# The second feed-forward matmul in seven groups of seven products, and low parts formed on GpSimd

## The chip, the core and the metric

The kernel runs on one core of a Trainium2 chip. Its engines work side by side, each through its own queue in order: TensorE (PE, its weight loads as PEld), VectorE (DVE), ScalarE (ACT), GpSimd (POOL) and SyncE (SP), which here issues the DMA transfers between main memory and the on-chip memory SBUF. TensorE accumulates into eight banks of a second memory, PSUM. The metric is device time in microseconds (us) of one execution; the time of a kernel is the median of its runs.

## What is computed

One layer over 512 positions of width 1024: a modulated norm, an input projection, two branches (a gated spatial mixing and a matrix-memory recurrence), their merge, an output projection, and then the part that the change touches:

```python
xn = modulate(rmsnorm(h, norm2_g[l]), sh2, sc2)
ff = jnp.square(jax.nn.relu(xn @ w_ff1[l])) @ w_ff2[l]
h = h + g2[:, None, :] * ff
...
return rmsnorm(h, final_g)
```

`w_ff2` has 4096 rows and 1024 columns. The second matmul is the product of the 512 x 4096 activations with it; its result is multiplied by the row `g2`, added to the residual, and the sum is normed and scaled by `final_g`.

## The kernel before

**Products in three parts.** Every f32 operand is split into a high part (a cast to fp32r, on ScalarE) and a low part (operand minus high part, on VectorE). `mm3` (lines 116 to 119) issues three matmuls: high by high, high by low, low by high. Of the tiles with names in the profile, `wh`/`wl` are the parts of weights and `hsh`/`hsl` those of activations.

**Groups.** The inner dimension of 4096 is cut into eight blocks of 512. `GROUPS = "WWWWWS"` (line 1013) says how the first six are done. The four quarters of the activations of block n are `hq[n, 0/1, 0/1]` (a11, a12, a21, a22, each 128 x 512 on chip), those of its weights are F11, F12, F21 and F22 (each 128 x 1024 on chip). A "W" block makes seven products of sums of quarters where the plain way makes eight; `passes` (lines 1103 to 1138) writes them out. For a W block it issues, beside the products, four sums of weights (lines 1115, 1123, 1127, 1131) and three of activations (1117 to 1119), all on VectorE. An "S" block makes the eight plain products in the same two passes. Pass 0 runs over all blocks and collects products P1, P2, P7 and P3, pass 1 runs over them again and collects P5, P6 and P4 (and, for the S block, E); the weight quarters that both passes need are loaded twice.

**A step** is one product: two rows of output by two inner slices by three matmuls, 12 matmuls with 512 columns each. For each step `hl` (lines 1091 to 1101) splits the activations, 128 x 512, and `w_pair` (1075 to 1086) the weights, 128 x 1024:

```python
act.copy(out=h_, in_=src)
dve.tensor_sub(out=l_, in0=src, in1=h_.bitcast(F32))
```

The loop at line 1206 calls `prefetch_step(5)`, so that the operands of five steps may be ready or under way. There are six buffers for split activations (after the first two), five for split weights and three or four for raw weights; a planner orders each engine's queue by estimated costs, within what the buffers allow.

**Collecting.** `after(key)` adds the collected products, which lie in PSUM, to `r` tiles in SBUF, on VectorE (lines 1181 to 1197). `gated` (1175 to 1179) multiplies an `r` tile by `g2` and adds it to the residual, two VectorE instructions of 128 x 512.

**The rest of the inner dimension,** rows 24 to 31 in units of 128 (`KF = 4 * NF` to `NK`), is done in plain pieces: `ff2_piece` loads one piece of 128 rows, ScalarE and VectorE split it, and `hs_pair` splits the matching activations. Four pieces are multiplied for all four row blocks at once (lines 1251 to 1258), with `gated` calls between them. The other four (`LAST = 4`) are kept and multiplied row block by row block in `mm_last` (1262), so that each row block can be finished (`add_out`, `square`, `scaled`, `root`, lines 1268 to 1304) while the next is multiplied. Row block 3 has its own ending (lines 1305 to 1328), whose upper half is cut into two parts of 256 columns.

**Elsewhere.** `evac_qk` (line 426), early in the kernel, is the one place before that forms a low part on GpSimd (line 439). The first feed-forward matmul (`product`, line 1000, and the sums behind it) runs just ahead of the stage. `load_split` (line 91) is the weight split of the earlier stages; its VectorE line is L96.

Of the kernel before, what the change touches and what calls it, by code (L numbers as in the profile page):

```python
# [8 lines left out]
F32 = mybir.dt.float32  # L9
F32R = mybir.dt.float32r  # L10
# [6 lines left out]
P = 128  # L17
D = 1024
T = 512
KT = D // P  # L20
TB = T // P
# [28 lines left out]
def block_kernel(ctx, tc, vecs_d, rows_d, ws_d, x_d, w_ada, w_in, w_out, w_ff1, w_ff2, out_d):  # L50
    nc = tc.nc
    act, dve, pool, pe, sp = nc.scalar, nc.vector, nc.gpsimd, nc.tensor, nc.sync
# [6 lines left out]
    def bank(nm):  # L59
        return psum.tile([P, 512], F32, tag="ps", name=nm)  # L60
# [55 lines left out]
    def mm3(out, ah, al, bh, bl, start, stop):  # L116
        pe.matmul(out, lhsT=ah, rhs=bh, start=start, stop=False)  # L117
        pe.matmul(out, lhsT=ah, rhs=bl, start=False, stop=False)  # L118
        pe.matmul(out, lhsT=al, rhs=bh, start=False, stop=stop)  # L119
# [487 lines left out]
    n = 0  # L607
# [182 lines left out]
    def halves(src, nm):  # L790
        hl = []
        for q in range(2):
            h_ = fp.tile([P, 512], F32R, tag="hT", name=f"{nm}h{q}", bufs=32)
            l_ = fp.tile([P, 512], F32R, tag="hT", name=f"{nm}l{q}", bufs=32)
            act.copy(out=h_, in_=src[q])
            dve.tensor_sub(out=l_, in0=src[q], in1=h_.bitcast(F32))
            hl.append((h_, l_))
        return hl
# [211 lines left out]
        prefetch_op(2)  # L1010
        return bk.rearrange("p (f t) -> p f t", f=2)

    GROUPS = "WWWWWS"

    def minus_a21(n):
        if GROUPS[n:n + 1] == "W":
# [74 lines left out]
    def hl(src):  # L1091
        i = count[1]
        count[1] += 1
        if i < 2:
            both = fp.tile([P, 2, 2, 256], F32R, tag="sc", name=f"hs0{i}", bufs=2)
            h_, l_ = both[:, 0], both[:, 1]
        else:
            h_, l_ = hs_tile("h"), hs_tile("l")
        act.copy(out=h_, in_=src)  # L1099
        dve.tensor_sub(out=l_, in0=src, in1=h_.bitcast(F32))  # L1100
        return h_, l_

    def passes():
# [55 lines left out]
    pass_pool.append(ps_stack.enter_context(tc.tile_pool(name="passes", bufs=1, side="right")))  # L1159
    for _ in range(4):  # L1160
        right.more()
    ws_ff = Stream([(w_ff2[k * P:(k + 1) * P, :], 1, D, f"f2{k}") for k in range(KF, NK - LAST)], 2)
    hsq = {}

    def hs_pair(kp):
        for th in range(2):
            hsq[kp, th] = hl(hq[kp // 2, kp % 2, th])
# [3 lines left out]
    def rtile(nm, t):  # L1171
        res[nm, t] = hsp.tile([P, 512], F32, name=f"r{nm}{t}")
        return res[nm, t]

    def gated(nm, t, row, hf):
        cs = slice(hf * 512, (hf + 1) * 512)
        r_ = res[nm, t]
        dve.tensor_mul(out=r_, in0=r_, in1=g2[:, cs])
        dve.tensor_add(out=xr[:, row, cs], in0=xr[:, row, cs], in1=r_)

    def after(key):
        for t in range(2):
            b_ = acc_b.get((key, t))
            if key == "P1":
                act.copy(out=rtile("1", t), in_=b_)
            elif key == "P7":
                dve.tensor_add(out=rtile("7", t), in0=res["1", t], in1=b_)
            elif key == "P3":
                dve.tensor_add(out=rtile("3", t), in0=res["1", t], in1=b_)
            elif key == "P2":  # L1190
                dve.tensor_add(out=res["1", t], in0=res["1", t], in1=b_)
            elif key == "P6":
                dve.tensor_add(out=res["3", t], in0=res["3", t], in1=b_)
                dve.tensor_add(out=res["7", t], in0=res["7", t], in1=b_)
            elif key == "P5":
                dve.tensor_add(out=res["3", t], in0=res["3", t], in1=b_)
                dve.tensor_add(out=rtile("5", t), in0=res["7", t], in1=b_)

    last_of = {key: max(i for i, p_ in enumerate(plan_) if p_[1] == key) for _, key in plan_}
    end0 = max(i for i, p_ in enumerate(plan_) if p_[0] == 0)  # L1200
    jobs = {}
    for i_, keys in ((last_of["P7"] + 2, ("P1", "P7")), (end0 + 2, ("P3", "P2")),
                     (last_of["P4"] if GROUPS[-1] == "W" else last_of["P6"] + 3, ("P6", "P5"))):
        jobs.setdefault(i_, []).extend(keys)
    NS = len(plan_)
    for i, (pas, key) in enumerate(plan_):
        prefetch_step(5)
        (h_, l_), (wh, wl) = ready.pop(0)
        first = (key, 0) not in acc_b
        for t in range(2):  # L1210
            if first:
                acc_b[key, t] = bank(f"g{key}{t}")
            ts_ = slice(t * P, (t + 1) * P)
            for j in range(2):
                mm3(acc_b[key, t], h_[:, j, ts_], l_[:, j, ts_], wh[:, j], wl[:, j], first and j == 0,
                    i == last_of[key] and j == 1 and key not in ("P4", "E"))
        for key_ in jobs.get(i, ()):
            after(key_)
        if i == end0:
            sp.dma_start(out=fing, in_=rows_d[5].partition_broadcast(P))  # L1220
        if NS - i <= 4:
            ws_ff.prefetch(max(0, 4 - (NS - i)))
        if i == NS - 2:
            hs_pair(KF // 2)

    ps_stack.close()
    lwp = ff.enter_context(tc.tile_pool(name="lwp", bufs=1, side="right"))
    o_banks = [[bank(f"ob{t}{hf}") for hf in range(2)] for t in range(2)]
    o_banks += [[acc_b["P4", t], acc_b["E", t]] for t in range(2)]
    late = [(nm, t, row + t, hf) for nm, row, hf in (("1", 0, 0), ("3", 0, 1), ("7", 2, 0), ("5", 2, 1)) for t in range(2)]  # L1230

    def ff2_piece(k, last=False):
        if last:
            raw = raws.tile([P, 1, D], F32, tag="raw", name=f"raw_f2{k}")
            sp.dma_start(out=raw[:, 0, :], in_=w_ff2[k * P:(k + 1) * P, :])
            wh = lwp.tile([P, 1, D], F32R, tag="lwh", name=f"wh_f2{k}", bufs=LAST)
            wl = lwp.tile([P, 1, D], F32R, tag="lwl", name=f"wl_f2{k}", bufs=LAST)
            act.copy(out=wh, in_=raw)
            dve.tensor_sub(out=wl, in0=raw, in1=wh.bitcast(F32))
        else:  # L1240
            wh, wl = ws_ff.next()
        if k % 2 == 0 and k > KF:
            hs_pair(k // 2)
        return wh, wl

    def mm_f2(k, t, hf, wh, wl, stop):
        cs = slice(hf * 512, (hf + 1) * 512)
        h_, l_ = (v[:, k % 2, (t % 2) * P:(t % 2 + 1) * P] for v in hsq[k // 2, t // 2])
        mm3(o_banks[t][hf], h_, l_, wh[:, 0, cs], wl[:, 0, cs], k == KF and t < 2, stop)

    for k in range(KF, NK - LAST):
        wh, wl = ff2_piece(k)
        for t in range(TB):
            for hf in range(2):
                mm_f2(k, t, hf, wh, wl, False)
        for _ in range(2):
            if late:
                gated(*late.pop(0))
    pcs = [ff2_piece(k, True) for k in range(NK - LAST, NK)]
    ss3 = fp.tile([P, TB, 3], F32, name="ss3")  # L1260
    rs3 = fp.tile([P, TB], F32, name="rs3")
    def mm_last(o, t, cs, start):
        for p_, (wh, wl) in enumerate(pcs):
            k_ = NK - LAST + p_
            h_, l_ = (v[:, k_ % 2, (t % 2) * P:(t % 2 + 1) * P] for v in hsq[k_ // 2, t // 2])
            mm3(o, h_, l_, wh[:, 0, cs], wl[:, 0, cs], start and p_ == 0, p_ == LAST - 1)

    def add_out(o, t, cs, nm):
        n = cs.stop - cs.start
        tmp = fp.tile([P, 512], F32, tag="tmp", name="ot" + nm, bufs=2)  # L1270
        dve.tensor_mul(out=tmp[:, 0:n], in0=o, in1=g2[:, cs])
        dve.tensor_add(out=xr[:, t, cs], in0=xr[:, t, cs], in1=tmp[:, 0:n])
# [1 line left out]
    def square(sc, t, cs, q):  # L1274
        act.activation(sc[:, cs], xr[:, t, cs], AF.Square, scale=1.0 / 32.0, accum_out=ss3[:, t, q:q + 1])

    def scaled(t, cs, nm):
        n = cs.stop - cs.start
        z = fp.tile([P, 512], F32, tag="hT", name="z" + nm, bufs=32)
        dve.tensor_mul(out=z[:, 0:n], in0=xr[:, t, cs], in1=fing[:, cs])  # L1280
        return z[:, 0:n]

    def root(t):
# [7 lines left out]
    for t in range(TB - 1):  # L1291
        sc = fp.tile([P, D], F32, tag="sc", name=f"sc3{t}", bufs=2)
        zs = []
        for hf, cs in enumerate((lo_, hi_)):
            mm_last(o_banks[t][hf], t, cs, False)
            add_out(o_banks[t][hf], t, cs, f"{hf}{t}")
            square(sc, t, cs, hf)
            if hf == 1:
                ss_sum(t)
            zs.append(scaled(t, cs, f"{hf}{t}"))  # L1300
        root(t)
        for z, cs in zip(zs, (lo_, hi_)):
            act.activation(xr[:, t, cs], z, AF.Copy, scale=rs3[:, t:t + 1])
            sp.dma_start(out=out_d[t * P:(t + 1) * P, cs], in_=xr[:, t, cs])
# [3 lines left out]
    mm_last(o_banks[t][0], t, lo_, False)  # L1308
    add_out(o_banks[t][0], t, lo_, "l0")
    square(sc, t, lo_, 0)  # L1310
    mm_last(o_banks[t][1][:, 0:256], t, c2, False)
    o_end = bank("obe")
    mm_last(o_end[:, 0:256], t, c3, True)
    add_out(o_banks[t][1], t, hi_, "l1")
    square(sc, t, c2, 1)
    ss_sum(t)
    add_out(o_end[:, 0:256], t, c3, "l2")
# [60 lines left out]
```

## Time and profile before

| what | value |
|---|---|
| time, median of 3 runs | 807.0 us (806.1 to 807.3) |
| the profiled execution | 806.75 us |
| its span in the profile | 805.0 us |
| TensorE busy, share of the span | 792.7 us, 98% |
| VectorE | 621.1 us, 77% |
| ScalarE | 404.2 us, 50% |
| GpSimd | 43.0 us, 5% |
| granted TensorE clock, mean | 0.994 of full |
| first matmul of the second feed-forward matmul | 636.03 us |
| last matmul of the kernel | 797.57 us |

Times in the profile count from the start of the span. A row in order of time has the start, the duration, the engine, the source line, the operation, "output <- inputs" by the program's names, the shapes, and how many such instructions it joins; in brackets the idle time before it and what ended it. A row of a group has the busy time and the mean duration in ns of one, and the idle time in front of them. Matmuls overlap, so that their spacing and not their duration gives their rate.

### The profile page before, as it was taken

The page shows a single profiled execution, that of the slowest core. Times are in us where ns is not written, and L with a number is a line of the kernel's source. Part 1 is how long each engine was busy: PE and PEld are TensorE (multiplying, and loading weights), DVE is VectorE, ACT ScalarE, POOL GpSimd, SP SyncE. Part 2 cuts the span into 40 slices and gives each one's busy share as a digit, 9 for nine tenths or more (in the row PEclk, how much of TensorE's full clock was granted, in tenths as well). Part 3 has the DMA queues.
Part 4 walks back from the last instruction along what each step waited for, and adds up shares of the span by engine and source line. Part 5 has one row for each costly group of instructions (what it writes and reads, how often), then busy time and mean ns, then how long its engine had stood idle before and what let it go on. Part 6 is the DMA issues. An engine that isn't in the chain of part 4 may idle for free.

```text
span 805.0 us, 11479 instructions
## 1 busy us (share of the span) xinstructions
PE 792.7 (98%) x4375; PEld 688.1 (85%) x4375; DVE 621.1 (77%) x938; ACT 404.2 (50%) x610; POOL 43.0 (5%) x62
## 2 busy tenths in 40 slices
PE   7999999999999999999999999999999999999996
PEld 6887888888988888888888899999999978888885
DVE  5889766774843348997847579888888799999966
ACT  5458566274533233242435247666666756646324
POOL 2004020121000000100000110000000000000000
PEclk8999999999999999999999999999999999999999
DMA  8974331143223388669337240333332466765302
GB/s 273 265 227 117 119 104 51 29 126 110 79 79 105 105 268 312 206 210 324 122 102 261 78 132 28 105 105 106 106 115 70 178 220 222 252 213 184 114 30 104
DMA packets 76423, 119.87 MB, mean 149 GB/s; under 512 B 5712, under 2 KB 38608, under 8 KB 76368
## 3 DMA queue, kind: packets, MB, share of 16 engines
q1 hardware_dynamic: 76368, 119.14, 46.6%
q8 instruction: 34, 0.56, 0.3%
q14 instruction: 21, 0.17, 0.1%
HBM read 117.02 MB, written 2.10 MB: 148 GB/s over the span
## 4 chain that ended last, share of the span: by engine, by line
PE 91%; DVE 2%; DMA 2%; ACT 2%; issue 1%; POOL 0%; SPq 0%; POOLq 0%; DVEq 0%
PE P L118 6%; PE P L117 6%; PE P L119 6%; PE gP L119 4%; PE gP L117 4%; PE gP L118 4%; PE qk L282 4%; PE wo L117 1%; PE wo L119 1%; PE wo L118 1%; PE cp L241 1%; PE k1b L117 1%; PE gb0b L118 1%; PE q1b L119 1%; PE gb0b L119 1%
## 5 line engine op out<-in xcount | busy, mean ns | idle before, releaser
L1099 ACT CAST hsh<-h 128x512 fp32r<-128x512 f32 x45 | 26.7, 620 | 26.9 <-PE gP L118 15.3
L1082 ACT CAST wh_g<-F 128x1024 fp32r<-128x1024 f32 x27 | 28.1, 1052 | 16.8 <-DVE F L1127 3.7
L119 PE MATMUL gP<-wh_g,hsl 128*128 128x512 f32 x92 | 35.8, 391 | 0.6 <-DVE hsl L1100 0.6
L118 PE MATMUL gP<-wl_g,hsh 128*128 128x512 f32 x92 | 35.8, 389 | 0.0
L117 PE MATMUL gP<-wh_g,hsh 128*128 128x512 f32 x92 | 35.7, 390 | 0.0
L1083 DVE TENSOR_TENSOR wl_g<-F,wh_g 128x1024 fp32r<-128x1024 f32 x27 | 32.9, 1225 | 0.8 <-ACT wh_g L1082 0.8
L921 ACT CAST wh_T<-T 128x1024 fp32r<-128x1024 f32 x21 | 22.0, 1048 | 20.0 <-PE P L118 18.4
L117 PE MATMUL P<-x2h,wh_B 128*128 128x256 f32 x112 | 31.6, 282 | 0.0
L118 PE MATMUL P<-x2l,wh_B 128*128 128x256 f32 x112 | 31.6, 282 | 0.0
L119 PE MATMUL P<-x2h,wl_B 128*128 128x256 f32 x112 | 31.6, 282 | 0.0
L921 ACT CAST wh_B<-B 128x1024 fp32r<-128x1024 f32 x21 | 22.0, 1049 | 16.4 <-PE P L118 15.4
L1100 DVE TENSOR_TENSOR hsl<-h,hsh 128x512 fp32r<-128x512 f32 x45 | 29.9, 692 | 0.3 <-ACT hsh L1099 0.3
L922 DVE TENSOR_TENSOR wl_T<-T,wh_T 128x1024 fp32r<-128x1024 f32 x21 | 25.7, 1224 | 3.0 <-ACT wh_T L921 2.9
L922 DVE TENSOR_TENSOR wl_B<-B,wh_B 128x1024 fp32r<-128x1024 f32 x21 | 25.6, 1220 | 0.0
L96 DVE TENSOR_TENSOR wl_gb<-raw_gb,wh_gb 128x1024 fp32r<-128x1024 f32 x8 | 9.8, 1224 | 19.7 <-ACT wh_gb L95 19.6
L118 PE MATMUL gP<-wl_x,hsh 128*128 128x512 f32 x64 | 24.9, 389 | 0.0
L117 PE MATMUL gP<-wh_x,hsh 128*128 128x512 f32 x64 | 24.9, 389 | 0.0
L119 PE MATMUL gP<-wh_x,hsl 128*128 128x512 f32 x64 | 24.9, 389 | 0.0
L667 DVE SCALAR_TENSOR_TENSOR accg<-arg,c_act,accg 128x1024 f32<-128x1024 f32 x14 | 18.0, 1283 | 6.5 <-DMA arg<-in_w_ada 6.3
L95 ACT CAST wh_ga<-raw_ga 128x1024 fp32r<-128x1024 f32 x8 | 8.4, 1052 | 27.2 <-PE ga0b L119 16.3
L976 ACT ACTIVATE h<-h 128x512 f32<-128x512 f32 x28 | 17.7, 632 | 8.5 <-DVE h L1036 4.0
L1082 ACT CAST wh_x<-F 128x1024 fp32r<-128x1024 f32 x16 | 16.6, 1050 | 9.5 <-DVE F L1115 3.9
(616 smaller groups left out, 2818.7 us busy)
## 6 DMA issues: line engine op xcount, KB each, us to landing
F<-in_w_ff SPq DMA_DIRECT2D x48, 512.0 KB, 4.2
B<-in_w_ff SPq DMA_DIRECT2D x28, 512.0 KB, 3.8
ar<-in_w_ada SPq DMA_DIRECT2D x64, 128.0 KB, 3.4
arg<-in_w_ada SPq DMA_DIRECT2D x16, 512.0 KB, 5.9
raw_f<-in_w_ff SPq DMA_DIRECT2D x12, 512.0 KB, 3.6
raw_o<-in_w_in SPq DMA_DIRECT2D x8, 512.0 KB, 4.1
raw_mv<-in_w_in SPq DMA_DIRECT2D x8, 512.0 KB, 3.6
raw_gb<-in_w_in SPq DMA_DIRECT2D x8, 512.0 KB, 3.7
```

What stands on the lines that cost most here:

```text
L117: pe.matmul(out, lhsT=ah, rhs=bh, start=start, stop=False)
L118: pe.matmul(out, lhsT=ah, rhs=bl, start=False, stop=False)
L119: pe.matmul(out, lhsT=al, rhs=bh, start=False, stop=stop)
L282: pe.matmul(bk, lhsT=wx[:, kk, f * P:(f + 1) * P], rhs=xx[k], start=k == 0 and ps_ == 0, stop=k == KT - 1 and ps_ == 2)
L667: dve.scalar_tensor_tensor(out=acc, in0=raw, scalar=c_act[:, k:k + 1], in1=acc, op0=ALU.mult, op1=ALU.add)
L921: act.copy(out=wh, in_=src)
L922: dve.tensor_sub(out=wl, in0=src, in1=wh.bitcast(F32))
L976: act.activation(dst, src, AF.Relu)
L1082: act.copy(out=wh, in_=src)
L1083: dve.tensor_sub(out=wl, in0=src, in1=wh.bitcast(F32))
L1099: act.copy(out=h_, in_=src)
L1100: dve.tensor_sub(out=l_, in0=src, in1=h_.bitcast(F32))
```

## The change

`GROUPS` becomes `"WWWWWWW"`: the sixth block becomes a W block, and rows 24 to 27 become a seventh. Only rows 28 to 31 stay as plain pieces. Their weights are loaded and split in the last five steps of the loop, by `last_piece`, as halves of 512 columns. The low part in `hl` is formed on GpSimd. The `gated` calls are placed anew: "1" some steps after pass 0, "3" on VectorE and "7" and "5" on GpSimd after the loop. The scaling with `final_g` of row blocks 1 and 2 goes to GpSimd too. P5 and P6 are collected after their own last steps. The bank E is no longer used; row blocks 2 and 3 take P4 and a new bank, and the row blocks 0 and 1 start on empty banks in `mm_last`. In row block 3, the upper half is added in two parts of 256 columns.

```diff
-    GROUPS = "WWWWWS"
+    GROUPS = "WWWWWWW"
...
         act.copy(out=h_, in_=src)
-        dve.tensor_sub(out=l_, in0=src, in1=h_.bitcast(F32))
+        pool.tensor_sub(out=l_, in0=src, in1=h_.bitcast(F32))
         return h_, l_
...
-    def gated(nm, t, row, hf):
+    def gated(nm, t, row, hf, eng=dve):
...
+    def last_piece(k):
+        raw = raws.tile([P, D], F32, tag="raw", name=f"raw_f2{k}")
+        sp.dma_start(out=raw, in_=w_ff2[k * P:(k + 1) * P, :])
+        return halves([raw[:, 0:512], raw[:, 512:1024]], f"f2{k}")
...
-                     (last_of["P4"] if GROUPS[-1] == "W" else last_of["P6"] + 3, ("P6", "P5"))):
+                     (last_of["P5"] + 1, ("P5",)), (last_of["P6"] + 1, ("P6",))):
...
-        if NS - i <= 4:
-            ws_ff.prefetch(max(0, 4 - (NS - i)))
-        if i == NS - 2:
-            hs_pair(KF // 2)
+        if NS - 5 <= i < NS - 5 + LAST:
+            pcs.append(last_piece(KF + i - (NS - 5)))
+        if i >= NS - 2:
+            hs_pair(KF // 2 + i - (NS - 2))
+        if i in (end0 + 4, end0 + 6):
+            gated("1", (i - end0) // 2 - 2, (i - end0) // 2 - 2, 0)
...
-    o_banks += [[acc_b["P4", t], acc_b["E", t]] for t in range(2)]
...
+    o_banks += [[acc_b["P4", t], bank(f"obr{t}")] for t in range(2)]
+    for t in range(2):
+        gated("3", t, t, 1)
+        gated("7", t, 2 + t, 0, pool)
+        gated("5", t, 2 + t, 1, pool)
...
-    def scaled(t, cs, nm):
+    def scaled(t, cs, nm, eng):
...
-            mm_last(o_banks[t][hf], t, cs, False)
+            mm_last(o_banks[t][hf], t, cs, t < 2 or hf == 1)
...
-            zs.append(scaled(t, cs, f"{hf}{t}"))
+            zs.append(scaled(t, cs, f"{hf}{t}", pool if t else dve))
...
-    add_out(o_banks[t][1], t, hi_, "l1")
+    add_out(o_banks[t][1][:, 0:256], t, c2, "l1")
```

`halves`, which `last_piece` calls, casts each half on ScalarE and forms its low part on VectorE, in tiles of the ring that holds the activations.

More of the change, by code (lines that the diff above doesn't have):

```diff
@@ L1161, in block_kernel @@
         right.more()
-    ws_ff = Stream([(w_ff2[k * P:(k + 1) * P, :], 1, D, f"f2{k}") for k in range(KF, NK - LAST)], 2)
     hsq = {}
@@ L1173, in rtile @@
         return res[nm, t]
-    def gated(nm, t, row, hf):
+    def gated(nm, t, row, hf, eng=dve):
         cs = slice(hf * 512, (hf + 1) * 512)
         r_ = res[nm, t]
-        dve.tensor_mul(out=r_, in0=r_, in1=g2[:, cs])
-        dve.tensor_add(out=xr[:, row, cs], in0=xr[:, row, cs], in1=r_)
+        eng.tensor_mul(out=r_, in0=r_, in1=g2[:, cs])
+        eng.tensor_add(out=xr[:, row, cs], in0=xr[:, row, cs], in1=r_)
+    pcs = []
+    def last_piece(k):
+        raw = raws.tile([P, D], F32, tag="raw", name=f"raw_f2{k}")
+        sp.dma_start(out=raw, in_=w_ff2[k * P:(k + 1) * P, :])
+        return halves([raw[:, 0:512], raw[:, 512:1024]], f"f2{k}")
     def after(key):
@@ L1191, in after @@
                 dve.tensor_add(out=res["1", t], in0=res["1", t], in1=b_)
-            elif key == "P6":
-                dve.tensor_add(out=res["3", t], in0=res["3", t], in1=b_)
-                dve.tensor_add(out=res["7", t], in0=res["7", t], in1=b_)
             elif key == "P5":
@@ L1197, in after @@
                 dve.tensor_add(out=rtile("5", t), in0=res["7", t], in1=b_)
+            elif key == "P6":
+                for nm in ("3", "7", "5"):
+                    dve.tensor_add(out=res[nm, t], in0=res[nm, t], in1=b_)
     last_of = {key: max(i for i, p_ in enumerate(plan_) if p_[1] == key) for _, key in plan_}
@@ L1215, in block_kernel @@
                 mm3(acc_b[key, t], h_[:, j, ts_], l_[:, j, ts_], wh[:, j], wl[:, j], first and j == 0,
-                    i == last_of[key] and j == 1 and key not in ("P4", "E"))
+                    i == last_of[key] and j == 1 and key != "P4")
         for key_ in jobs.get(i, ()):
@@ L1220, in block_kernel @@
             sp.dma_start(out=fing, in_=rows_d[5].partition_broadcast(P))
-        if NS - i <= 4:
-            ws_ff.prefetch(max(0, 4 - (NS - i)))
-        if i == NS - 2:
-            hs_pair(KF // 2)
+        if NS - 5 <= i < NS - 5 + LAST:
[4 more added lines that the diff above has]
+            gated("1", (i - end0) // 2 - 2, (i - end0) // 2 - 2, 0)
     ps_stack.close()
-    lwp = ff.enter_context(tc.tile_pool(name="lwp", bufs=1, side="right"))
     o_banks = [[bank(f"ob{t}{hf}") for hf in range(2)] for t in range(2)]
-    o_banks += [[acc_b["P4", t], acc_b["E", t]] for t in range(2)]
[L1230 to L1259, printed above, removed]
+    o_banks += [[acc_b["P4", t], bank(f"obr{t}")] for t in range(2)]
[3 more added lines that the diff above has]
+        gated("5", t, 2 + t, 1, pool)
     ss3 = fp.tile([P, TB, 3], F32, name="ss3")
@@ L1262, in mm_last @@
     def mm_last(o, t, cs, start):
-        for p_, (wh, wl) in enumerate(pcs):
-            k_ = NK - LAST + p_
+        hf, c0 = cs.start // 512, cs.start % 512
+        part = slice(c0, c0 + cs.stop - cs.start)
+        for p_ in range(LAST):
+            k_ = KF + p_
             h_, l_ = (v[:, k_ % 2, (t % 2) * P:(t % 2 + 1) * P] for v in hsq[k_ // 2, t // 2])
-            mm3(o, h_, l_, wh[:, 0, cs], wl[:, 0, cs], start and p_ == 0, p_ == LAST - 1)
+            wh, wl = pcs[p_][hf]
+            mm3(o, h_, l_, wh[:, part], wl[:, part], start and p_ == 0, p_ == LAST - 1)
     def add_out(o, t, cs, nm):
@@ L1275, in square @@
         act.activation(sc[:, cs], xr[:, t, cs], AF.Square, scale=1.0 / 32.0, accum_out=ss3[:, t, q:q + 1])
-    def scaled(t, cs, nm):
+    def scaled(t, cs, nm, eng):
         n = cs.stop - cs.start
         z = fp.tile([P, 512], F32, tag="hT", name="z" + nm, bufs=32)
-        dve.tensor_mul(out=z[:, 0:n], in0=xr[:, t, cs], in1=fing[:, cs])
+        eng.tensor_mul(out=z[:, 0:n], in0=xr[:, t, cs], in1=fing[:, cs])
         return z[:, 0:n]
@@ L1310, in block_kernel @@
     square(sc, t, lo_, 0)
-    mm_last(o_banks[t][1][:, 0:256], t, c2, False)
+    mm_last(o_banks[t][1][:, 0:256], t, c2, True)
     o_end = bank("obe")
     mm_last(o_end[:, 0:256], t, c3, True)
-    add_out(o_banks[t][1], t, hi_, "l1")
+    add_out(o_banks[t][1][:, 0:256], t, c2, "l1")
     square(sc, t, c2, 1)
```

## The prediction

> **What bounds the kernel now.** The page comes first, for the span and for the engines.
>
> ```profile
> span 805.0 us, 11479 instructions
> ...
> PE 792.7 (98%) x4375; PEld 688.1 (85%) x4375; DVE 621.1 (77%) x938; ACT 404.2 (50%) x610; POOL 43.0 (5%) x62
> ```
>
> The shares are means over stages with different limits, so the stages of the second feed-forward matmul come next, as busy time of each engine in three stretches (PE, PEld, DVE, ACT, POOL, then granted clock, DMA share, GB/s).
>
> ```profile
> 660.00:700.00 40.00, 40.00 (x178) 33.11 (x177) 39.97 (x48) 26.14 (x35) 0.00 (x0) 1.00 0.66 213
> 700.00:740.00 40.00, 40.00 (x178) 33.07 (x177) 39.71 (x44) 23.20 (x29) 0.00 (x0) 1.00 0.61 196
> 740.00:772.00 32.00, 32.00 (x143) 26.50 (x142) 31.81 (x44) 12.82 (x15) 0.00 (x0) 1.00 0.37 132
> ```
>
> TensorE and VectorE are both full here, GpSimd does nothing, and the clock is whole. To see which of the two sets the pace, their rates are needed, from the order of time on TensorE and on VectorE (start, duration, instruction).
>
> ```profile
> 641.50 0.39 PE L117 MATMUL gP<-wh_g,hsh 128*128 128x512 f32 x1
> ...
> 649.66 0.39 PE L117 MATMUL gP<-wh_g,hsh 128*128 128x512 f32 x1
> ...
> 797.57 0.28 PE L119 MATMUL obe<-wh_f,hsl 128*128 128x256 f32 x1
> ```
>
> ```profile
> 640.24 1.23 DVE L1083 TENSOR_TENSOR wl_x<-F,wh_x 128x1024 fp32r<-128x1024 f32 x1 [0.27 <-ACT wh_x L1082]
> 642.00 1.23 DVE L1115 TENSOR_TENSOR F<-F,F 128x1024 f32<-128x1024 f32 x1 [0.54 <-DMA F<-in_w_ff]
> ...
> 656.50 1.90 DVE L1100 TENSOR_TENSOR hsl<-h,hsh 128x512 fp32r<-128x512 f32 x3
> 658.31 1.23 DVE L1115 TENSOR_TENSOR F<-F,F 128x1024 f32<-128x1024 f32 x1
> ...
> 738.13 2.36 DVE L1083 TENSOR_TENSOR wl_x<-F,wh_x 128x1024 fp32r<-128x1024 f32 x2
> 740.40 0.69 DVE L1100 TENSOR_TENSOR hsl<-h,hsh 128x512 fp32r<-128x512 f32 x1
> ...
> 746.86 0.69 DVE L1196 TENSOR_TENSOR r<-r,gP 128x512 f32<-128x512 f32 x1
> 747.46 0.69 DVE L1197 TENSOR_TENSOR r<-r,gP 128x512 f32<-128x512 f32 x1
> ```
>
> Between the first two TensorE rows lie three steps of 12 matmuls: 8.16 us, so 2.72 us a step and 0.2267 us a matmul. On VectorE three 128x512 forms take 658.31 - 656.50 = 1.81 us, 0.603 each; two 128x1024 forms 740.40 - 738.13 = 2.27 us, 1.135 each; an addition that reads PSUM 0.60. A "W" group of seven products issues 7 weight low parts (1024 wide), 4 weight sums (1024), 3 activation sums (512) and 7 activation low parts (512): 11 x 1.135 + 10 x 0.603 = 18.5 us of VectorE against 84 x 0.2267 = 19.04 us of TensorE. TensorE sets the pace by half a microsecond a group. The groups of VectorE from 642 to 772 us show the low parts that the change moves (L1100), each 0.692 us from start to end, behind the others:
>
> ```profile
> L1083 DVE TENSOR_TENSOR wl_g<-F,wh_g 128x1024 fp32r<-128x1024 f32 x24 | 29.2, 1225 | 0.3 <-ACT wh_g L1082 0.3
> L1100 DVE TENSOR_TENSOR hsl<-h,hsh 128x512 fp32r<-128x512 f32 x43 | 28.6, 692 | 0.0
> L1083 DVE TENSOR_TENSOR wl_x<-F,wh_x 128x1024 fp32r<-128x1024 f32 x15 | 18.3, 1223 | 0.0
> L1115 DVE TENSOR_TENSOR F<-F,F 128x1024 f32<-128x1024 f32 x5 | 6.1, 1229 | 0.5 <-DMA F<-in_w_ff 0.5
> ```
>
> **The change part by part.** *Matmuls.* The sixth group goes from eight products to seven (96 matmuls to 84), and rows 24 to 27 of the inner dimension, four plain pieces of 24 matmuls, become a seventh group (96 to 84). That takes 24 x 0.2267 = 5.4 us from TensorE.
>
> *VectorE without GpSimd's part.* A group keeps 11 x 1.135 + 3 x 0.603 = 14.3 us. Two more groups of this kind are to be prepared in place of the lighter eight-product group and the plain pieces. By itself that would fit well under 19.04.
>
> *GpSimd's low parts.* The stage has no GpSimd instruction before, but the kernel uses the same form (two f32 inputs of 128x512 in SBUF, fp32r out) earlier, at L439, beside VectorE low parts of the same form as L1083. In order of time, GpSimd and then VectorE:
>
> ```profile
> 71.94 1.30 POOL L439 TENSOR_TENSOR q2l<-yb,q2h 128x512 fp32r<-128x512 f32 x1 [1.49 <-ACT q2h L438]
> ...
> 75.79 1.29 POOL L439 TENSOR_TENSOR k0l<-yb,k0h 128x512 fp32r<-128x512 f32 x1 [1.29 <-ACT k0h L438]
> 77.64 1.67 POOL L439 TENSOR_TENSOR k1l<-yb,k1h 128x512 fp32r<-128x512 f32 x1 [0.56 <-ACT k1h L438]
> ```
>
> ```profile
> 68.32 5.99 DVE L433 SCALAR_TENSOR_TENSOR yb<-qk,vecs,yb 128x511 f32<-128x511 f32 x9
> ...
> 76.16 2.00 DVE L96 TENSOR_TENSOR wl_o<-raw_o,wh_o 128x1024 fp32r<-128x1024 f32 x1
> 78.08 2.31 DVE L96 TENSOR_TENSOR wl_k<-raw_k,wh_k 128x1024 fp32r<-128x1024 f32 x1
> ```
>
> These rows decide the case. The subtraction at 76.16 starts while GpSimd is at k0l (until 77.08) and takes 2.00 us, not 1.22. GpSimd's k1l, begun at 77.64 under it, takes 1.67 us, not 1.30: it ends 1.15 us after VectorE's at 78.16. The subtraction at 78.08 then takes 2.31 us and ends 1.08 us after k1l at 79.31. The two take turns; none runs beside the other. The nine L433 forms, which read one operand from PSUM, ran at 0.67 us each beside q2l at 1.30: with these there is no exclusion. So a GpSimd low part costs VectorE 2.31 - 1.22 = 1.09 us, where VectorE itself needed 0.603: the move costs 0.49 us of VectorE's queue each time, it saves nothing. Bounds: below 0, if GpSimd always finds VectorE at a PSUM read or waiting; above 1.30, its whole duration. I take 1.09, since nearly every VectorE form in this stage reads two SBUF operands and the third stretch above leaves 0.2 us of 32 idle.
>
> The page "SBUF — State Buffer" of the Trainium skill, in its section "Who interferes with whom", says that a VectorE instruction with two SBUF inputs and a GpSimd instruction that reads SBUF hold a shared port in turn, each for its whole instruction. The rows agree on the turns; for the whole instruction they show 1.09 to 1.15 us, not 1.30. By the page the price would be 1.30 and the sum below 13 us longer.
>
> A group is then 14.3 + 7 x 1.09 = 21.9 us on VectorE against 19.04 on TensorE: 2.9 us late, seven times.
>
> *The sum along VectorE.* In the trace of before the row at 640.24 ends the weights of the fourth step (the first pair of the "x" kind), so steps 0 to 3 are prepared when VectorE starts L1115 at 642.0; it is busy from there on. Still to do of the 49 steps: 45 weight low parts and 28 weight sums, 73 x 1.135 = 82.9; 21 activation sums, 12.7; 45 GpSimd low parts, 45 x 1.09 = 49.1; six PSUM additions (P7, P3, P2), 3.6; the early residual update "1" (two rows, two forms each), 2.4. Together 150.7: the last step is ready at 792.7, while TensorE, at its sixth step at 649.66, would start it 43 steps of 2.72 us later, near 767.
>
> Behind it stand: eight halves of the last weights (`last_piece`), 4.8; the four `hs_pair` low parts on GpSimd, 4.4; the P5 and P6 additions, 10 x 0.60 = 6.0; update "3" on VectorE, 2.4; updates "7" and "5" on GpSimd, 8 x 1.09 = 8.7; rows 0 to 2 of the end (three pairs of product and sum, row 0's two scalings and three small sums), 8.9; the scalings of rows 1 and 2, now on GpSimd, 4 x 1.09 = 4.4. That is 39.6, to 832.3. What GpSimd does beside the 22 PSUM reads (13.2 us) costs nothing; I credit half, 6.6, since ten of them stand in a row before the updates that wait for them: 825.7 (bounds 819.1 and 832.3).
>
> The last row then takes VectorE two forms of 0.60, five steps of about 0.34 or less up to its last sum, and what follows that sum as before:
>
> ```profile
> 797.88 0.42 DVE L1271 TENSOR_TENSOR otl<-obe,rowg 128x256 f32<-128x256 f32 x1
> 798.22 0.42 DVE L1320 TENSOR_TENSOR zl<-yb,fing 128x256 f32<-128x256 f32 x1
> 798.56 0.15 DVE L1287 SCALAR_TENSOR_TENSOR rs<-ss 128x1 f32<-128x1 f32 x1
> 798.63 0.42 DVE L1272 TENSOR_TENSOR yb<-yb,otl 128x256 f32<-128x256 f32 x1
> ```
>
> 1.2 + 4 x 0.34 + 0.07 = 2.6, and 805.0 - 798.63 = 6.4: 9.0. The span comes to 834.7 (828 to 841). The profiled execution took 806.75, 1.75 more than its span, and the median of the runs is 0.25 above it: 836.7.
>
> *At nothing.* Eight weight loads of 512 KB for the seventh group replace four pieces, 2 MB more; they go through the SyncE queue behind the same ring of three buffers, with the DMA engines at 0.37 to 0.66 in the stretches above; if that cover were gone, the last load of 512 KB would show as a wait on F, 0.54 us as at 642.0. ScalarE's casts are the same in a group and it is busy 26 of 40 us. The narrower last sum of row 3 (256 wide) frees 0.26 us of VectorE that was hidden by TensorE, whose last matmul starts at 797.57.
>
> **The rivals.** *A: GpSimd slips in beside VectorE.* Place: the 49 steps. If GpSimd's average block is under (19.04 - 14.3) / 7 = 0.68 us, VectorE keeps up, TensorE stays the bound and the change gives its 5.4 us: 807.0 - 5.4 = 801.6, faster. For it: PSUM reads do not exclude it, and a VectorE without its seven low parts may wait for ScalarE, where GpSimd runs free. Against: waits of VectorE for ScalarE are 0.3 us in the L1083 row, and every overlap of two SBUF forms quoted shows the full block.
>
> *B: part of the blocks is hidden.* With 0.85 us on average, 61 GpSimd forms (45 + 4 + 8 + 4) cost 61 x 0.24 = 14.6 us less: about 822.
>
> *C: only the preparation is late.* If the planner puts the late updates where VectorE has time, TensorE ends the kernel: the last pieces are ready 7 x 0.603 + 3 x 1.09 = 7.5 after 792.7, TensorE starts some 2 us before that, takes 96 x 0.2267 = 21.8, and from the end of its last product (797.57 and half of 0.2267) to 805.0 follow 7.3: 827.3, with the 2.0 outside the span 829.
>
> *D: the block is the whole duration,* 1.30: 61 x 0.21 = 12.8 more, 849.5. The 2.31 row speaks against it. It is what the page of the Trainium skill named above would give.
>
> **How the numbers follow.** The forecast has 0.60, C 0.16, B 0.10, A 0.09, D 0.05. A measurement of this kernel cannot tell less than 0.2% from no change. Faster is A, 0.09; within 0.2%, 0.02 of B, with a block near the 0.68 that decides; the rest, 0.89, is slower. The range takes in the forecast's bounds (830 to 843 as a run), C, most of B and a little above: 814 to 846, leaving out A, D and the tail of B.
>
> **What would show it.** The page shows some 24 matmuls fewer. Right: L1100 on POOL with 1.7 us or more in many of its rows, L1083 with a mean well above 1.225 us, TensorE idle in front of the low parts by some 20 us and a step of 3.1 us in place of 2.72; VectorE later than TensorE at the end. Wrong: L1083 still at 1.22 us beside a busy POOL (A), or TensorE full to its last matmul. What would overturn the sum most is VectorE idling in the stage while GpSimd works.

## The result, and the profile after

The changed kernel takes 837.1 us (median of 4 runs, 836.7 to 839.5) against 806.6 us before: the ratio is 1.0388, with an interval of 1.0362 to 1.0414. The profiled execution took 836.72 us, its span is 834.9 us. The page of the changed kernel, its span, engines and costliest groups:

```profile
span 834.9 us, 11560 instructions
...
PE 794.9 (95%) x4351; PEld 683.7 (82%) x4351; DVE 649.0 (78%) x903; ACT 408.2 (49%) x622; POOL 162.3 (19%) x127
...
L1100 POOL TENSOR_TENSOR hsl<-h,hsh 128x512 fp32r<-128x512 f32 x51 | 99.1, 1965 | 73.4 <-ACT hsh L1099 72.8
...
L1083 DVE TENSOR_TENSOR wl_g<-F,wh_g 128x1024 fp32r<-128x1024 f32 x30 | 46.1, 1543 | 0.5 <-ACT wh_g L1082 0.5
```

TensorE has its 24 matmuls fewer (4351 for 4375). VectorE has 35 instructions fewer and is busy 28 us longer: the weight low part L1083, 1225 ns before, has a mean of 1543 ns. The low part on GpSimd has a mean of 1965 ns in its records, its waiting for VectorE included. The busy time by stage (columns as in the prediction's table of stages):

```profile
640.00:660.00 20.00, 15.81 (x65) 12.01 (x64) 15.40 (x16) 11.24 (x14) 10.38 (x5) 0.97 0.78 259
660.00:680.00 20.00, 20.00 (x85) 16.39 (x84) 17.25 (x14) 9.04 (x13) 13.55 (x9) 0.94 0.42 136
...
720.00:740.00 20.00, 12.72 (x45) 9.63 (x45) 20.00 (x16) 9.56 (x13) 15.94 (x8) 0.83 0.54 176
740.00:760.00 20.00, 19.82 (x88) 16.08 (x86) 20.00 (x16) 8.48 (x11) 10.21 (x7) 1.00 0.63 189
760.00:780.00 20.00, 15.16 (x60) 10.87 (x60) 19.96 (x13) 8.90 (x11) 9.79 (x6) 1.00 0.58 184
```

From 720 to 780 us VectorE is full, and TensorE is short of work in two of the three stretches. In the first two stretches shown VectorE isn't full either: it waits. VectorE in order of time shows both things, the wait and the turns, and then the end:

```profile
640.30 2.32 DVE L1115 TENSOR_TENSOR F<-F,F 128x1024 f32<-128x1024 f32 x1
...
656.62 1.22 DVE L1115 TENSOR_TENSOR F<-F,F 128x1024 f32<-128x1024 f32 x1
662.72 0.69 DVE L1117 TENSOR_TENSOR h<-h,h 128x512 f32<-128x512 f32 x1 [4.88 <-POOL hsl L1100]
...
704.27 2.31 DVE L1083 TENSOR_TENSOR wl_x<-F,wh_x 128x1024 fp32r<-128x1024 f32 x1
706.51 2.31 DVE L1123 TENSOR_TENSOR F<-F,F 128x1024 f32<-128x1024 f32 x1
...
792.00 2.33 DVE L1083 TENSOR_TENSOR wl_x<-F,wh_x 128x1024 fp32r<-128x1024 f32 x1
...
825.07 0.68 DVE L1255 TENSOR_TENSOR otl<-gP,rowg 128x512 f32<-128x512 f32 x1
```

At 704.27 and 706.51 two forms (instructions of one shape) that take 1.22 us undisturbed take 2.31 us each: 1.09 us more, the length read from the early stage before the change. At 662.72 VectorE had stood still for 4.88 us. L1117 writes a21 in place, and a21 is what GpSimd was still reading for its low part. The list of waits between 642 and 830 us (instruction waited in, releaser: us in total, times, longest) has this and, on TensorE, waits for VectorE's and GpSimd's low parts and one for VectorE's L1193:

```profile
DVE h L1117 <- POOL hsl L1100: 7.3, 2, 4.9
...
PE gP L117 <- DVE r L1193: 6.7, 1, 6.7
PE gP L118 <- DVE wl_x L1083: 5.8, 7, 1.5
...
PE gP L118 <- DVE wl_g L1083: 4.7, 4, 2.6
...
PE gP L119 <- POOL hsl L1100: 2.8, 2, 2.5
...
DVE F L1115 <- DMA F<-in_w_ff: 2.3, 2, 1.2
```

TensorE in order of time, from its first step to its last matmul:

```profile
634.49 0.40 PE L117 MATMUL gP<-wh_g,hs 128*128 128x512 f32 x1
...
656.12 0.39 PE L118 MATMUL gP<-wl_g,hsh 128*128 128x512 f32 x1
659.02 0.79 PE L119 MATMUL gP<-wh_g,hsl 128*128 128x512 f32 x1 [2.52 <-POOL hsl L1100]
659.61 0.63 PE L117 MATMUL gP<-wh_g,hsh 128*128 128x512 f32 x1
660.04 0.63 PE L118 MATMUL gP<-wl_g,hsh 128*128 128x512 f32 x1
...
725.53 0.39 PE L119 MATMUL gP<-wh_x,hsl 128*128 128x512 f32 x1
732.59 0.80 PE L117 MATMUL gP<-wh_x,hsh 128*128 128x512 f32 x1 [6.68 <-DVE r L1193]
...
796.99 0.39 PE L117 MATMUL ob<-f228h,hsh 128*128 128x512 f32 x1
...
819.17 0.28 PE L119 MATMUL obe<-f231h,hsl 128*128 128x256 f32 x1
```

The 49 steps take (796.99 - 634.49) / 49 = 3.32 us each, where TensorE by itself takes 2.72. TensorE is done at 819.17; VectorE comes to the last row only at 825.07.

### The profile page after: what moved, and what is told of

It reads as the page before. It is cut to its first block, busy times and chain, and to the rows that moved or that the text cites. A ratio compares the mean times of both kernels' runs of the same rounds, so it can differ in the third digit from the quotient of the medians.

```text
span 834.9 us, 11560 instructions
## 1 busy us (share of the span) xinstructions
PE 794.9 (95%) x4351; PEld 683.7 (82%) x4351; DVE 649.0 (78%) x903; ACT 408.2 (49%) x622; POOL 162.3 (19%) x127
## 4 chain that ended last, share of the span: by engine, by line
PE 74%; DVE 16%; issue 4%; DMA 3%; ACT 2%; POOL 1%; SPq 0%; POOLq 0%; DVEq 0%; ACTq 0%
PE P L119 6%; PE P L117 6%; PE P L118 6%; PE qk L282 4%; DVE wl_g L1083 3%; DVE wl_x L1083 2%; PE wo L117 2%; PE wo L119 2%; PE wo L118 2%; DVE F L1123 1%; DMA F<-in_w_ff 1%; DVE F L1131 1%; PE cp L241 1%; PE f10b L118 1%; DVE F L1127 1%
## 5 line engine op out<-in xcount | busy, mean ns | idle before, releaser
L1100 POOL TENSOR_TENSOR hsl<-h,hsh 128x512 fp32r<-128x512 f32 x51 | 99.1, 1965 | 73.4 <-ACT hsh L1099 72.8
L118 PE MATMUL gP<-wl_g,hsh 128*128 128x512 f32 x112 | 44.9, 401 | 4.7 <-DVE wl_g L1083 4.7
L119 PE MATMUL gP<-wh_g,hsl 128*128 128x512 f32 x112 | 44.8, 400 | 2.8 <-POOL hsl L1100 2.8
L1083 DVE TENSOR_TENSOR wl_g<-F,wh_g 128x1024 fp32r<-128x1024 f32 x30 | 46.1, 1543 | 0.5 <-ACT wh_g L1082 0.5
L117 PE MATMUL gP<-wh_g,hsh 128*128 128x512 f32 x112 | 44.2, 395 | 0.0
L117 PE MATMUL gP<-wh_x,hsh 128*128 128x512 f32 x76 | 30.8, 405 | 6.7 <-DVE r L1193 6.7
L118 PE MATMUL gP<-wl_x,hsh 128*128 128x512 f32 x76 | 31.3, 412 | 5.8 <-DVE wl_x L1083 5.8
L1083 DVE TENSOR_TENSOR wl_x<-F,wh_x 128x1024 fp32r<-128x1024 f32 x19 | 31.2, 1643 | 1.8 <-ACT wh_x L1082 1.8
L118 PEld LDWEIGHTS gP<-wl_g,hsh 128*128 128x128 f32 x112 | 21.3, 191 | 12.0 <-DVE wl_g L1083 7.6
L119 PEld LDWEIGHTS gP<-wh_g,hsl 128*128 128x128 f32 x112 | 21.4, 191 | 8.2 <-POOL hsl L1100 4.0
```

The lines of the kernel that those rows point to most:

```text
L1083: dve.tensor_sub(out=wl, in0=src, in1=wh.bitcast(F32))
L1100: pool.tensor_sub(out=l_, in0=src, in1=h_.bitcast(F32))
```

## The experiments

The theory: GpSimd's reading forms and VectorE's forms with two SBUF inputs take turns, and VectorE pays for it. (The time by which one GpSimd form lengthens a VectorE form is called a block below.) The rivals: the groups and the late additions are the cost; the load of GpSimd, whatever it does, is the cost; the new wait of L1117 is the cost. Each ratio is against the kernel before on the same chip.

### The changed kernel with the activation low parts on VectorE

```diff
-        pool.tensor_sub(out=l_, in0=src, in1=h_.bitcast(F32))
+        dve.tensor_sub(out=l_, in0=src, in1=h_.bitcast(F32))
```

> The changed kernel with only the activation low parts (45 after 642 us) back on VectorE. Theory (GpSimd and VectorE take turns): each costs VectorE 0.603 instead of 1.09 us, the preparation of the last step ends near 642 + 129 = 771 instead of 794, TensorE is the bound up to there; the end still has twelve GpSimd forms: 808 to 816 us. Rival, seven groups are too much for VectorE whoever forms the low parts: 830 us or more.

Measured: 815.5 us, ratio 1.0118 (1.0075 to 1.0161), at the upper edge of what was expected. Groups of VectorE from 642 to 810 us:

```profile
L1083 DVE TENSOR_TENSOR wl_g<-F,wh_g 128x1024 fp32r<-128x1024 f32 x27 | 33.1, 1225 | 0.0
...
L1100 DVE TENSOR_TENSOR hsl<-h,hsh 128x512 fp32r<-128x512 f32 x49 | 34.2, 723 | 0.0
```

VectorE has 49 more forms to do and L1083 is back at 1225 ns. Between this kernel and the changed one lie 1.0388 - 1.0118 = 0.027, 21.8 us, for this one line: over two thirds of the loss of 31 us. What is left is still 1.2% slower than before.

### The kernel before with only the low parts moved

```diff
-        dve.tensor_sub(out=l_, in0=src, in1=h_.bitcast(F32))
+        pool.tensor_sub(out=l_, in0=src, in1=h_.bitcast(F32))
```

> The kernel before with only the activation low parts moved to GpSimd; six groups, plain pieces and late updates as they were. Theory: 43 forms after 642 us cost 0.49 us more each on a VectorE that was full until 771.8, 21 us, of which up to 7 us hide in its idle time after that: 818 to 828 us. Rival, seven groups are the cause: 807 us, no change.

Measured: 829.3 us, ratio 1.0291 (1.0268 to 1.0314), 24.1 us more and just above the range expected. Of the groups of VectorE from 642 to 835 us, L1083 goes from 1225 to 1717 ns:

```profile
L1083 DVE TENSOR_TENSOR wl_g<-F,wh_g 128x1024 fp32r<-128x1024 f32 x24 | 40.9, 1717 | 0.0
```

The move is dear without the seven groups too. Over the 43 forms after 642 us it is 0.56 us each, where the prediction had 1.09 - 0.603 = 0.49 for a form that goes from one queue into the way of the other. The 0.56 is a net figure: in this kernel too VectorE waits for GpSimd at L1117 (6.1 us) and for DMA before its sums (3.8 us).

### GpSimd as busy, but writing and not reading

```diff
-        pool.tensor_sub(out=l_, in0=src, in1=h_.bitcast(F32))
+        pool.tensor_sub(out=l_[:, 0, 0:1], in0=src[:, 0, 0:1], in1=h_[:, 0, 0:1].bitcast(F32))
+        pool.memset(l_.bitcast(F32), 0.0)
+        pool.memset(l_.bitcast(F32), 0.0)
+        pool.tensor_sub(out=l_[:, 0, 0:1], in0=src[:, 0, 0:1], in1=h_[:, 0, 0:1].bitcast(F32))
```

> The changed kernel, but in place of each activation low part GpSimd does a subtraction of one column, two fills of the whole tile with zeros (a fill reads nothing) and the one column again; the low parts are left out of the result. GpSimd keeps a similar busy time per step, all its waits and all who wait for it stay. Theory (it is the reading that takes turns): VectorE's weight low parts back at 1.22 us, the stage bound by TensorE, 801 to 812 us. Rival, the waits between the engines are the cause (VectorE's L1117 waits for GpSimd 7.3 us, ScalarE for L1118): 828 to 837 us.

Measured: 812.1 us, ratio 1.0078 (1.0050 to 1.0106), just above the range. Groups from 642 to 810 us, of VectorE and then of GpSimd:

```profile
L1083 DVE TENSOR_TENSOR wl_g<-F,wh_g 128x1024 fp32r<-128x1024 f32 x27 | 32.9, 1220 | 2.2 <-ACT wh_g L1082 2.2
...
L1120 DVE TENSOR_TENSOR h<-h,h 128x512 f32<-128x512 f32 x7 | 4.8, 691 | 10.5 <-POOL hsl L1103 10.3
```

```profile
L1100 POOL TENSOR_TENSOR hsl<-h,hsh 128x1 fp32r<-128x1 f32 x49 | 36.6, 749 | 23.8 <-ACT hsh L1099 23.8
L1101 POOL MEMSET hsl<- 128x512 f32 x49 | 25.8, 526 | 2.1
```

GpSimd is busy for about 109 us here (36.6 + 25.8, the second fill 25.7 and the second column 21.2), more than the 94 us that the records of the real low parts have from 642 to 830 us in the changed kernel, waiting included, and VectorE's weight low parts aren't stretched. The wait of L1117, here L1120, is even longer (10.3 us), and yet 25 us are gone. So GpSimd's load isn't what costs, nor a wait there by itself; what went with the 25 us is the reads of 128 x 512. What that wait costs where VectorE is full is asked by the run without it, below.

### The kernel before with an extra reading form, and with an extra filling one

Both write into a tile that nobody reads, once for each activation split but the first two.

```diff
+        if i >= 2:
+            dum = hsp.tile([P, 2, 256], F32, tag="dum", name=f"dum{i}", bufs=1)
+            pool.tensor_sub(out=dum, in0=src, in1=h_.bitcast(F32))
```

> The kernel before, with one more GpSimd subtraction per activation split (128x512, the same inputs, into a tile that nothing reads). Theory: 1.09 us of VectorE for each of 45, 49 us less up to 7 us of idle time: 840 to 856 us. Rival, only waits between the engines count: nobody waits for it, 805 to 812 us.

```diff
+        if i >= 2:
+            dum = hsp.tile([P, 2, 256], F32, tag="dum", name=f"dum{i}", bufs=1)
+            pool.tensor_sub(out=dum[:, 0, 0:1], in0=src[:, 0, 0:1], in1=h_[:, 0, 0:1].bitcast(F32))
+            pool.memset(dum, 0.0)
+            pool.memset(dum, 0.0)
```

> The kernel before with extra GpSimd work per activation split as in the run with the extra subtraction, but work that reads almost nothing: one column subtracted, then two fills of 128x512. Theory (only a GpSimd instruction that reads SBUF takes turns with VectorE): 805 to 812 us against 846 for the subtraction. Rival, any GpSimd work slows VectorE: 825 us or more.

Measured: the reading form 846.0 us, ratio 1.0505 (1.0464 to 1.0546); the filling one 809.7 us, ratio 1.0041 (1.0026 to 1.0056), both inside their ranges. The groups of VectorE, first with the reading form (642 to 835 us), then with the filling one (642 to 780 us):

```profile
L1100 DVE TENSOR_TENSOR hsl<-h,hsh 128x512 fp32r<-128x512 f32 x43 | 44.6, 1060 | 0.0
...
L1083 DVE TENSOR_TENSOR wl_g<-F,wh_g 128x1024 fp32r<-128x1024 f32 x24 | 35.5, 1487 | 0.0
```

```profile
L1083 DVE TENSOR_TENSOR wl_g<-F,wh_g 128x1024 fp32r<-128x1024 f32 x24 | 29.0, 1217 | 0.2 <-ACT wh_g L1082 0.2
L1100 DVE TENSOR_TENSOR hsl<-h,hsh 128x512 fp32r<-128x512 f32 x43 | 28.3, 682 | 0.0
```

This takes the price of a block with VectorE's work unchanged: 40.9 us over 43 reading forms after 642 us, 0.95 us each, net of what VectorE's idle time hid, and 3.5 us over the whole kernel for the fills. The section "Who interferes with whom" of the page "SBUF — State Buffer" in the Trainium skill says that a VectorE instruction with two SBUF inputs collides with a GpSimd instruction that reads SBUF and not with one that only writes it. These two runs agree, 1487 against 1217 ns.

### The changed kernel with nothing of the change on GpSimd

```diff
-        pool.tensor_sub(out=l_, in0=src, in1=h_.bitcast(F32))
+        dve.tensor_sub(out=l_, in0=src, in1=h_.bitcast(F32))
...
-        gated("7", t, 2 + t, 0, pool)
-        gated("5", t, 2 + t, 1, pool)
+        gated("7", t, 2 + t, 0)
+        gated("5", t, 2 + t, 1)
...
-            zs.append(scaled(t, cs, f"{hf}{t}", pool if t else dve))
+            zs.append(scaled(t, cs, f"{hf}{t}", dve))
```

> The changed kernel with all that it gave to GpSimd back on VectorE: low parts, late updates and scalings. What is left is the change of the groups alone. Theory: each of the twelve forms still on GpSimd in the run with the low parts on VectorE (815.5 us) costs up to 0.49 us more there, so 809 to 815 us: still slower than before, since seven groups of 18.5 us, ten additions and the updates stand in VectorE's queue to the end. Rival, the groups alone gain their 5.4 us: 800 to 803 us.

Measured: 813.2 us, ratio 1.0081 (1.0050 to 1.0111), inside the range. Its stages, and VectorE's first form of the last row:

```profile
740.00:780.00 40.00, 38.88 (x165) 30.11 (x164) 40.00 (x49) 21.21 (x29) 0.00 (x0) 1.00 0.47 159
780.00:800.00 20.00, 16.48 (x85) 13.94 (x83) 20.00 (x36) 4.56 (x12) 1.10 (x2) 0.97 0.07 27
```

```profile
802.26 0.68 DVE L1255 TENSOR_TENSOR otl<-gP,rowg 128x512 f32<-128x512 f32 x1
```

The groups alone make the kernel slower by 0.8%, with no GpSimd in the way. VectorE has no idle time between its first sum at 642.16 and 802.26, and TensorE's last matmul starts at 796.21, while VectorE still has rows to finish. The prediction's own terms give this: 123.7 us of VectorE's own work and 61 x 0.603 = 36.8 for the forms that return make 160.5; measured 802.26 - 642.16 = 160.1. The matmuls saved 5.4 us of TensorE; the group and halves that replace the plain pieces put more on VectorE, which was within half a microsecond a group of being the bound already. The late updates and scalings on GpSimd (first experiment against this one, 1.0118 and 1.0081) can't be told from no difference: the intervals overlap.

### The changed kernel without its wait at L1117

The a21 of pass 0 is split on VectorE, ahead of the sum that overwrites it; the other low parts stay on GpSimd.

```diff
-    def hl(src):
+    def hl(src, eng=pool):
...
-        pool.tensor_sub(out=l_, in0=src, in1=h_.bitcast(F32))
+        eng.tensor_sub(out=l_, in0=src, in1=h_.bitcast(F32))
...
-                    yield hl(a21), w_pair(b12, right)
+                    yield hl(a21, dve), w_pair(b12, right)
```

> The changed kernel with the low part of one activation quarter in seven (a21, the one that VectorE's L1117 overwrites) back on VectorE, so that L1117 waits for no GpSimd form. If the wait only stood in place of blocks: 7 times 0.49 us, 832 to 835 us. If the wait of 7.3 us comes on top of the blocks: 824 to 828 us.

Measured: 836.0 us, ratio 1.0363 (1.0337 to 1.0390), against 1.0388 (1.0362 to 1.0414) with the wait. The intervals overlap, and the time lies just above the 832 to 835 us expected if the wait stood in place of blocks, far from the 824 to 828 us expected if it came on top of them. The stretch where the wait stood, in this kernel and then in the changed one:

```profile
642.00:660.00 18.00, 16.47 (x73) 13.29 (x73) 17.97 (x18) 8.77 (x13) 8.56 (x4) 1.00 0.76 266
```

```profile
642.00:660.00 18.00, 13.81 (x56) 10.35 (x55) 13.40 (x15) 10.18 (x13) 8.85 (x4) 0.97 0.75 243
```

VectorE is full there now, 17.97 us for 13.40, and TensorE does 73 matmuls where it did 56. By the same working as in the table below, its idle time up to the last row falls from 13.4 to 7.1 us, but the blocks don't fall with the seven forms fewer on GpSimd (45.8 us over 54 forms, for 46.0 over 61), and these seven are back in VectorE's queue, 7 x 0.603 = 4.2 us. From the first sum to the last row that leaves 2.3 us; as the first sum comes 1.0 us later here (641.27 for 640.30), the spans differ by 1.3 us (833.6 for 834.9).

### The kernel before with six W groups

Nothing on GpSimd, plain pieces and updates as before, but the sixth block by seven products, so 12 matmuls fewer.

```diff
-    GROUPS = "WWWWWS"
+    GROUPS = "WWWWWW"
```

The banks of row blocks 2 and 3 are P4 and a new one, as in the change.

> The kernel before with its eight-product group made a seven-product group and nothing else (plain pieces and GpSimd as before). TensorE loses 12 matmuls, 2.7 us; VectorE gets 18.5 in place of 11.5 us, 7.0 more, of which its idle time after 771.8 us hides some. Theory (VectorE is nearly full, a saved matmul is worth less than its sums): 805 to 810 us. Rival, TensorE is the bound: 802 to 803 us.

Measured: 806.3 us, ratio 0.9990 (0.9972 to 1.0008), inside the range: no difference. The last matmul of TensorE in this kernel, and VectorE where the plain pieces end, in it and in the kernel before:

```profile
797.57 0.28 PE L119 MATMUL obe<-wh_f,hsl 128*128 128x256 f32 x1
```

```profile
780.29 0.69 DVE L1271 TENSOR_TENSOR ot<-ob,rowg 128x512 f32<-128x512 f32 x1 [1.12 <-PE ob L119]
```

```profile
778.69 0.69 DVE L1271 TENSOR_TENSOR ot<-ob,rowg 128x512 f32<-128x512 f32 x1 [6.56 <-PE ob L119]
```

The 2.7 us taken from TensorE are gone by its last matmul, which starts at 797.57 as before. Some 0.6 us of them is a later start of the stage (636.59 for 636.03); the rest went into short gaps between its matmuls, 2.7 us in all for 0.8 before. VectorE comes to the first finished row with 1.12 us to spare instead of 6.56: the sixth group took most of the room that it had.

## Why the prediction was right, and where its terms were not

The forecast was 836.7 us; the profiled execution took 836.72. The sum along VectorE, term by term:

| term | predicted | measured |
|---|---|---|
| start of the sum (L1115) | 642.0 | 640.3 |
| VectorE's own work to the last row | 123.7 | 125.4 |
| GpSimd's forms in its way | 66.6 - 6.6 = 60.0 | 46.0 |
| idle | 0 | 13.4 |
| first form of the last row | 825.7 | 825.07 |
| from there to the end | 9.0 | 9.8 |
| span | 834.7 | 834.9 |

The 46.0 is what the rows of VectorE from 640.30 to 825.07 last beyond the 1.22 us (1024 wide) and 0.68 us (512 wide) that the same forms take where GpSimd is idle, over 47 rows that exceed it. The 13.4 is the idle time between these rows. The own work is the rest of the 184.8 us. The prediction took its start from the trace of before; here the whole stage began earlier (first matmul 634.49 for 636.03). In the traces of all the kernels here it lies between 634.5 and 637.5, so these 1.7 us can't be put down to the change.

**The mechanism holds.** Turns at 1.09 us each are seen at 704.27 and 706.51 and give L1083 its 1543 ns; the experiments with reading and filling forms tie them to the reads.

**The term "GpSimd's low parts" was mis-sized, and the sum lacked a wait.** The prediction let GpSimd find VectorE at a form with two SBUF inputs nearly every time and credited only the PSUM reads. The blocks came to 46.0 us, not 60.0. But VectorE idled for 13.4 us, where the sum has none: 7.3 us before L1117, 3.4 us for DMA (2.3 us before L1115 and 1.1 us before L1123), the rest in small pieces. The prediction had named VectorE idling while GpSimd works as what would overturn the sum most; it happened, and the two errors cancelled. While VectorE waits for GpSimd, GpSimd blocks nobody. 46.0 + 13.4 = 59.4 took the place of 60.0, and the early start made up for 1.7 us more of own work, so the agreement to a few tenths is luck. That the time came out near the forecast is not all luck: without the wait at L1117 the stretch was filled, the forms left blocked for 0.85 us each instead of 0.75, and the time stayed within about a microsecond.

**Rival A was priced from a bound that the change itself shifts.** It gave 801.6 us if GpSimd's work were free. With free-running fills in place of reads it was 812.1, and with nothing of it on GpSimd 813.2. A's 5.4 us hold where TensorE stays the bound to the end, and it did not: in both VectorE began the last row after TensorE's last matmul had started, at 800.37 against 798.38 and at 802.26 against 796.21.

**Rival C** had TensorE end the kernel; VectorE began the last row 5.9 us after TensorE's last matmul started (825.07 - 819.17). **D**, a whole block of 1.30, would have made the two rows at 704 and 706 us 2.5 us long; they took 2.31. **B**, with 0.85 a form: the blocks alone, 46.0 us over 61 forms, were 0.75, below even this, and only the idle time brought the time back to the forecast.

**Smaller steps.** A step was to take 3.1 us, it took 3.32. TensorE was to stand some 20 us in front of low parts; it stood 13.3 us (5.8 + 4.7 for VectorE's, 2.8 for GpSimd's). The last step's weights were to be ready at 792.7; they were at 792.00 + 2.33 = 794.3. The weight loads, costed at nothing, show as the DMA waits above, up to 1.2 us each, more than the 0.54 given for lost cover. That these come from the seventh group's loads is not shown: the kernel with nothing on GpSimd has the same loads and no such wait after its first sum, and the kernel before with the low parts moved has six groups and waits 3.8 us. What sets them off stays open.

**What was not foreseen and did not decide.** TensorE waited 6.68 us for a PSUM bank at 725.53: pass 0 now ends in a W group, and the bank of P7 comes free only with VectorE's addition L1193, which stood behind the blocked forms. With the low parts back on VectorE this wait was 0.2 us. That it did not decide is read from VectorE, which was full in this stretch.

## What to carry to other kernels

A form moved to an idle engine is only cheaper if the engine it leaves isn't held up by it: count its price in the old engine's queue (here 1.09 against 0.603 us), not in the new one's idle time. Before saving matmuls by sums of operands, add up the other engine's work on the same stretch, to its last instruction; half a microsecond of slack a group does not carry another group. A moved read also moves the release of its input: look for what overwrites that tile in place.

## What the runs showed of the hardware that was not expected

**GpSimd does not always get the next turn.** VectorE in the kernel with the extra reading form, in order of time, and GpSimd at the same time:

```profile
723.57 1.21 DVE L1083 TENSOR_TENSOR wl_g<-F,wh_g 128x1024 fp32r<-128x1024 f32 x1
724.71 0.68 DVE L1100 TENSOR_TENSOR hsl<-h,hsh 128x512 fp32r<-128x512 f32 x1
...
733.92 0.68 DVE L1192 TENSOR_TENSOR r<-r,gP 128x512 f32<-128x512 f32 x1
734.59 1.63 DVE L1083 TENSOR_TENSOR wl_x<-F,wh_x 128x1024 fp32r<-128x1024 f32 x1
```

```profile
723.71 11.43 POOL L1103 TENSOR_TENSOR dum<-h,hsh 128x512 f32<-128x512 f32 x1 [8.09 <-ACT hsh L1099]
```

Its first form here is recorded from 723.71 for 11.43 us, while VectorE's forms follow each other at their usual length; it ends at 735.14, 1.2 us after the read of PSUM at 733.92 began. By their records, 61 of the 63 GpSimd forms of 128 x 512 between 636 and 830 us in the changed kernel got in at once or when the VectorE form then running ended; the other two waited past two or three more. What decides this stays open.

**A gap of 2.7 us was followed by half of TensorE's rate.** After the gap that ends at 659.02, 2.67 us beyond the usual spacing, matmuls stand 0.43 us apart (659.61, 660.04) instead of 0.227 until 662.2; after the one that ends at 732.59 it lasted about 4.4 us. The granted clock, the third number from the right, is 0.50 in the first of these stretches of the changed kernel:

```profile
659.00:662.20 3.20, 3.18 (x8) 2.50 (x9) 0.00 (x0) 0.92 (x1) 3.20 (x3) 0.50 0.50 182
```

That page of the Trainium skill which treats it, "TensorE: Matmul & The Clock Gate", Part 1, puts the gate at an idle window of about 3.4 us; here a gap of 2.67 us was followed by the half rate, for 3.2 us. The loss, some 0.2 us a matmul, fell on TensorE, which waited for VectorE's low parts later all the same.
